# Depthwise convolution block as diagonal matmuls, an fp32 value product on column halves, and shifted loads and stores in a two-layer hybrid trunk

## The chip, the cores and the metric

One core of a Trainium2 chip runs the whole kernel. The metric is device microseconds of one execution. TensorE is PE, its weight loads PEld, VectorE DVE, ScalarE ACT, GpSimd POOL; SP is the queue that issues most DMAs.

## What is computed

Two layers over 1024 tokens of width 1024. Each normalizes, projects once into four mixers, gates each mixer's output, projects back, adds the residual and a gated embedding. The parts that matter here, cut from the reference:

```python
def nsa_attention(q, kc, vc, k_sel, v_sel, k_win, v_win, gates, rel_bias):
    ...
    p_c = masked_softmax(s_c, d_c >= 0)
    o_c = jnp.einsum('bhqn,bnd->bqhd', p_c, vc)
    ...
    o_s = jnp.einsum('bhqm,bqmd->bqhd', p_s, vsel.reshape(B, Q_BLOCK, -1, dk))
    ...
    o_w = jnp.einsum('bhqk,bkd->bqhd', p_w, vw)
    o = gc[..., 0:1] * o_c + gc[..., 1:2] * o_s + gc[..., 2:3] * o_w

def conv_module(a, b, w_dw, b_dw, ln_g, ln_b, w_pw, b_pw):
    x = a * jax.nn.sigmoid(b)
    y = lax.conv_general_dilated(x, w_dw[:, None, :].astype(x.dtype), window_strides=(1,),
                                 padding=((CONV_WIDTH - 1, 0),),
                                 dimension_numbers=('NWC', 'WIO', 'NWC'),
                                 feature_group_count=C) + b_dw
    y = jax.nn.silu(layer_norm(y, ln_g, ln_b))
    return y @ w_pw + b_pw
```

Attention has 4 heads of 64 channels; the convolution has 256 channels and 31 taps. The other mixers are a spatial gating unit and an RWKV-7 recurrence. All is float32.

## The kernel before

Everything is held channel-major, 128 channels by 512 tokens to a tile, and each layer is worked off in two halves of 512 tokens, each half in 4 attention tiles of 128 tokens. `ORDER` (line 32) is written out by hand: one string of steps for each layer and half, run by `run`. The steps that matter: `R` and `r` are the RWKV chunk solve and its serial steps, `N` prepares attention (`nsa_front`, which compresses keys and values in `compress_in` and `compress_out`), `A` is one attention tile, `T` the convolution's taps, `C` what follows them, `O` the output projection, `e` the embedding. The framework's scheduler then interleaves these steps on each engine by priority, within what tiles and PSUM banks allow.

**Dense products** (`mm3`, line 168) are three matmuls over a high and a low part of both operands, in the rounded type that the rows call fp32r. `split_w` (line 150) makes the two parts of each 128x512 piece of weights: ACT rounds it (line 161), POOL subtracts (line 163), and the low part is stored in DRAM (line 165), so that the next half loads it (line 160) and spares POOL.

**The convolution's taps** (`conv_taps`, line 686) run wholly on DVE: for each of two blocks of 128 channels one multiply-add with bias (line 692) and 30 multiply-accumulates (line 695) over 512 tokens. `conv_out` then takes the layer norm's sums on PE as plain fp32 matmuls (line 705), which PE runs as two instructions each.

**An attention tile** (`attn_tile`, line 923; scores and softmax in `branch`, line 987) transposes the probabilities into PSUM tile `pt` (line 969), copies them rounded (ACT, line 972), takes the rest of the rounding (DVE, line 973), and multiplies both with value tiles that hold the high and the low part of v side by side, 128 columns (lines 978 and 979). The two halves of the PSUM tile `pv` are then added (lines 981 and 982) and the gate is multiplied in (line 985). Tiles `pt`, `pv`, `rp` and `c` have one PSUM bank each, `mm` and `s` two.

**DMA issue** is on SP for nearly all: the weights (line 155), the stored low parts, the compression's weights (line 865, 8 loads of 256 KB in each half), the recurrence's state between chunks (line 537, into one buffer `x0`, read by the add of line 551), the embedding's product on its way to DRAM (`ped`, line 1076), and the output (line 1139).

Of the kernel before, what the change touches and what calls it, by code (L numbers as in the profile page):

```python
# [41 lines left out]
class Trunk:  # L42
    def __init__(self, ctx, tc, a):
# [8 lines left out]
        self.low = {}  # L52
        self.setup()

    BUFS = {"aT": 16, "ws": 3, "wh": 3, "wl": 3, "t2": 7, "y": 7, "rv": 2, "pt": 4, "r4": 2, "ab": 8,
# [94 lines left out]
    def split_w(self, src, cols, key):  # L150
        nc = self.nc
        with self.tc.high_priority(offset=4000):
# [9 lines left out]
            if kept is None:  # L162
                nc.gpsimd.tensor_sub(lo[:, :cols], st[:, :cols], hi[:, :cols].bitcast(F32))  # L163
                kept = self.low[key] = self.dram.tile([128, cols], F32, name=f"low{len(self.low)}")
                nc.sync.dma_start(kept, lo[:, :cols].bitcast(F32))
# [8 lines left out]
    def w_granule(self, w2d, k0, nk, segs):  # L174
# [8 lines left out]
        hi, lo = self.split_w(src, nk * n, (w2d.tensor.name, w2d.offset, k0, nk, tuple(segs)))  # L183
# [347 lines left out]
    def rwkv_tri(self, c):  # L531
# [4 lines left out]
        XY = self.t([128, 256], "x0", bufs=1)  # L536
# [149 lines left out]
    def conv_taps(self):  # L686
        nc = self.nc
        par, cw, xg = self.par, self.cw, self.xg
        acc = []
        for j in range(2):  # L690
            ac = self.t([128, 544], "cv")[:, :TH]
            nc.vector.tensor_scalar(ac, xg[j][:, 0:TH], cw[:, j * 31:j * 31 + 1], par[:, P_CB + j:P_CB + j + 1],
# [102 lines left out]
    def nsa_front(self):  # L795
        nc = self.nc
        h = self.h
        im = self.compress_in()
# [14 lines left out]
        VS = self.t([128, NT, 2, 2, 64], "vs", bufs=2, dt=F32R)  # L813
        pv4 = pv.rearrange("p (t s d) -> p t s d", t=NT, s=2)
        nc.scalar.copy(VS[:, :, :, 0, :], pv4)
        nc.vector.tensor_sub(VS[:, :, :, 1, :], pv4, VS[:, :, :, 0, :].bitcast(F32))
# [11 lines left out]
        self.compress_out(*im)  # L828

# [28 lines left out]
    def compress_out(self, im, ns, nn):  # L858
        nc, h = self.nc, self.h
        ph = self.ps("pt")  # L860
        w1 = self.a["nsa_w1"][self.l]
        for kv in range(2):
            for g in range(4):
                w = self.t([128, TH], "ld")
                nc.sync.dma_start(w.rearrange("p (l m) -> p l m", l=4),
                                  w1[kv, g * 512:g * 512 + 512].rearrange("(l p) m -> p l m", p=128))
                for i in range(4):
                    nc.tensor.matmul(ph[32 * i:32 * i + 32, kv * 128:kv * 128 + 128], im[kv][:, g * 4 + i],  # L868
                                     w[:, i * 128:i * 128 + 128], start=(g == 0), stop=(g == 3))
# [28 lines left out]
        self.VC = self.t([128, 2, 64], "vc", bufs=2, dt=F32R)  # L898
        nc.scalar.copy(self.VC[0:64, 0], pt[0:64, 0:64])
        nc.vector.tensor_sub(self.VC[0:64, 1], pt[0:64, 0:64], self.VC[0:64, 0].bitcast(F32))  # L900
        nc.scalar.copy(self.VC[64:128], self.VC[0:64].bitcast(F32))
# [21 lines left out]
    def attn_tile(self, w, t, za):  # L923
# [27 lines left out]
        CS = self.t([128, TH], "pt", dt=F32R)  # L951
        nc.scalar.copy(CS[0:64], pt[0:64])
        nc.vector.tensor_sub(CS[64:128], pt[0:64], CS[0:64].bitcast(F32))
        for hp in range(2):
            pv = self.ps("pv")
            acc = pv[:, :256]
            vc = w.VC.rearrange("p a b -> p (a b)")
            nc.tensor.matmul(acc, vc, CS[:, hp * 256:hp * 256 + 256], start=True, stop=False)
            for br in range(2):
# [3 lines left out]
                for b in range(b0, i + 1, 2):  # L963
# [7 lines left out]
                    Th, Tl = self.t([128, TH], "pt", dt=F32R), self.t([128, TH], "pt", dt=F32R)  # L971
                    nc.scalar.copy(Th[:, :n], pt[:, :n])  # L972
                    nc.vector.tensor_sub(Tl[:, :n], pt[:, :n], Th[:, :n].bitcast(F32))  # L973
                    for x in range(nb):
                        hh, tt = divmod(b + x, NT)
                        vs = w.VS[hh][:, tt, br].rearrange("p a b -> p (a b)")
                        last = br == 1 and b + x == i
                        nc.tensor.matmul(acc, vs, Th[:, x * 256:x * 256 + 256], start=False, stop=False)  # L978
# [343 lines left out]
```

## Time and profile before

| | |
|---|---|
| median of 3 runs | 1896.93 us (1891.67 to 1896.95) |
| the profiled execution | 1898.52 us |
| its span on the core | 1896.8 us, 1.7 us less than its time |
| mean granted clock of PE | 0.93 of 2.4 GHz |
| busy share PE, DVE, ACT, POOL | 89%, 69%, 43%, 20% |
| instructions PE, DVE, ACT, POOL | 9444, 3457, 1837, 311 |

A busy share counts overlapping matmuls as they show in the trace, where each lies some 0.2 us under the next, so PE's share overstates its load: the distance between the starts of neighbours (the pitch) tells what one costs. DMA engines are 50.6% busy with 148 GB/s over the span.

### The profile page before, as it was taken

Reading aid. Unit: us, or ns where it says so; the run is one execution under the profiler, and the core shown is the slowest. Engines: PE = TensorE matmul, PEld = TensorE weight load, DVE = VectorE, ACT = ScalarE, POOL = GpSimd, SP = SyncE. Lnnn points to the kernel's source line nnn. Section 1 sums busy time; section 2 is a strip of 40 time slices with the busy share of each in tenths; the row PEclk is TensorE's granted clock in tenths of the full one; section 3 lists DMA queues with packets and bytes.
Section 4 is the critical chain, followed back from the end, with each engine's and each line's share of the span. In section 5 each row is a group of like instructions: output and inputs, shape, how many; then the busy total and the mean of one; then the engine's idle time right before and its main releaser. Section 6 shows DMA issues by size and latency. Waiting matters only on the chain. (4 is left out here: it accounts for less than half of the span.)

```text
span 1896.8 us, 28498 instructions
## 1 busy us (share of the span) xinstructions
PE 1692.2 (89%) x9444; PEld 1267.9 (67%) x9444; DVE 1306.3 (69%) x3457; ACT 813.4 (43%) x1837; POOL 375.9 (20%) x311
## 2 busy tenths in 40 slices
PE   4886898899799999989968989899988999989998
PEld 3564576677576777767645768676766767667676
DVE  3456689787787756777666883568768876486562
ACT  4332233454333455545322334455532435555553
POOL 2222234000001142312222331200000112422231
PEclk7888799899898999989987989899998989989999
DMA  7456454334664354633364438673365525335566
GB/s 244 101 151 144 126 167 134 99 96 105 168 198 118 85 178 153 212 114 106 110 139 126 146 119 253 200 227 91 109 171 166 148 73 178 116 123 167 164 216 208
DMA packets 382283, 282.16 MB, mean 149 GB/s; under 512 B 94764, under 2 KB 307760, under 8 KB 382136
## 3 DMA queue, kind: packets, MB, share of 16 engines
q1 hardware_dynamic: 382136, 280.34, 50.6%
q8 instruction: 74, 1.21, 0.3%
q14 instruction: 73, 0.60, 0.1%
HBM read 195.72 MB, written 84.54 MB: 148 GB/s over the span
## 5 line engine op out<-in xcount | busy, mean ns | idle before, releaser
L170 PE MATMUL mm<-aT,wh 128*128 128x512 f32 (+1 forms) x1304 | 539.8, 416 | 5.0 <-ACT aT L258 2.8
L171 PE MATMUL mm<-aT,wh 128*128 128x512 f32 (+1 forms) x1304 | 534.9, 411 | 2.7 <-DVE aT L259 2.5
L172 PE MATMUL mm<-aT,wl 128*128 128x512 f32 (+1 forms) x1304 | 535.9, 411 | 1.1 <-DMA wl<-low 1.1
L161 ACT CAST wh<-ws 128x512 fp32r<-128x512 f32 (+2 forms) x388 | 237.1, 612 | 440.0 <-PE mm L171 240.1
L163 POOL TENSOR_TENSOR wl<-ws,wh 128x512 fp32r<-128x512 f32 (+1 forms) x212 | 282.9, 1336 | 697.1 <-ACT wh L161 599.3
L170 PEld LDWEIGHTS mm<-aT,wh 128*128 128x128 f32 (+1 forms) x1304 | 251.6, 193 | 56.5 <-ACT aT L258 4.8
L171 PEld LDWEIGHTS mm<-aT,wh 128*128 128x128 f32 (+1 forms) x1304 | 252.3, 193 | 51.5 <-DVE aT L259 7.7
L172 PEld LDWEIGHTS mm<-aT,wl 128*128 128x128 f32 (+1 forms) x1304 | 251.0, 192 | 49.4 <-DMA wl<-low 1.7
L695 DVE SCALAR_TENSOR_TENSOR cv<-cv,cw,cv 128x512 f32<-128x512 f32 x240 | 191.9, 815 | 3.3
L973 DVE TENSOR_TENSOR pt<-pt,pt 128x512 fp32r<-128x512 f32 (+1 forms) x152 | 94.1, 619 | 99.4 <-ACT pt L972 98.3
L1036 ACT ACTIVATE r<-s,sma 128x512 f32<-128x512 f32 (+3 forms) x192 | 106.0, 554 | 81.7 <-DVE sma L1034 42.2
L972 ACT CAST pt<-pt 128x512 fp32r<-128x512 f32 (+1 forms) x152 | 80.2, 527 | 97.8 <-PE pt L969 97.3
L609 POOL TENSOR_TENSOR q<-SB,gc 128x256 f32<-128x256 f32 x28 | 24.4, 871 | 431.3 <-DMA Xd<-q 152.3
L969 PE MATMUL pt<-cst,r 128*128 128x128 f32 x528 | 98.5, 284 | 12.5 <-DVE r L1041 10.0
L969 PEld LDWEIGHTS pt<-cst,r 128*128 128x128 f32 x528 | 65.5, 145 | 39.3 <-DVE r L1041 18.1
L979 PE MATMUL pv<-pt,vs 128*128 128x256 f32 x264 | 80.3, 322 | 7.8 <-DVE pt L973 7.5
L978 PE MATMUL pv<-pt,vs 128*128 128x256 f32 x264 | 85.7, 325 | 1.1 <-ACT pt L972 0.7
L1006 PE MATMUL s<-kv,qs 128*128 128x512 f32 (+2 forms) x192 | 77.1, 402 | 6.1 <-ACT r L1036 5.8
L979 PEld LDWEIGHTS pv<-pt,vs 128*128 128x128 f32 x264 | 51.4, 195 | 32.9 <-DVE pt L973 27.1
L1041 DVE TENSOR_SCALAR r<-r,sma 128x640 f32<-128x640 f32 (+7 forms) x128 | 72.2, 564 | 0.9
L978 PEld LDWEIGHTS pv<-pt,vs 128*128 128x128 f32 x264 | 51.6, 195 | 31.5 <-ACT pt L972 25.3
L868 PE MATMUL pt<-ld,t 128*32 128x128 f32 x256 | 12.8, 325 | 64.6 <-DMA ld<-in_nsa_w_dram 63.8
(337 smaller groups left out, 2863.8 us busy)
## 6 DMA issues: line engine op xcount, KB each, us to landing
ws<-in_w_in_dram SPq DMA_DIRECT2D x232, 256.0 KB, 3.2
low<-wl SPq DMA_DIRECT2D x200, 256.0 KB, 2.1
wl<-low SPq DMA_DIRECT2D x172, 256.0 KB, 2.8
ws<-in_ple_gate_dram SPq DMA_DIRECT2D x64, 256.0 KB, 3.0
ws<-in_w_out_dram SPq DMA_DIRECT2D x60, 256.0 KB, 3.0
ped<-ot SPq DMA_DIRECT2D x32, 256.0 KB, 3.8
ld<-in_nsa_w_dram SPq DMA_DIRECT2D x32, 256.0 KB, 3.4
ld<-ped SPq DMA_DIRECT2D x32, 256.0 KB, 3.9
```

The source lines that it names most:

```text
L161: nc.scalar.copy(hi[:, :cols], st[:, :cols])
L163: nc.gpsimd.tensor_sub(lo[:, :cols], st[:, :cols], hi[:, :cols].bitcast(F32))
L170: nc.tensor.matmul(out, lh, rh, start=first, stop=False, skip_group_check=shared)
L171: nc.tensor.matmul(out, lh, rl, start=False, stop=False, skip_group_check=shared)
L172: nc.tensor.matmul(out, ll, rh, start=False, stop=last, skip_group_check=shared)
L695: nc.vector.scalar_tensor_tensor(ac, xg[j][:, k:k + TH], cw[:, j * 31 + k:j * 31 + k + 1], ac, op0=OP.mult, op1=OP.add)
L969: nc.tensor.transpose(pt[:, o:o + 128], P[e][:, (b + x - b0) * 128:(b + x - b0) * 128 + 128], self.ident)
L972: nc.scalar.copy(Th[:, :n], pt[:, :n])
L973: nc.vector.tensor_sub(Tl[:, :n], pt[:, :n], Th[:, :n].bitcast(F32))
L978: nc.tensor.matmul(acc, vs, Th[:, x * 256:x * 256 + 256], start=False, stop=False)
L979: nc.tensor.matmul(acc, vs, Tl[:, x * 256:x * 256 + 256], start=False, stop=last)
L1036: nc.scalar.activation(P[:, o:o + wd], p[:, c:c + wd], AF.Exp, bias=ng[:, 0:1], accum_out=den[:, x:x + 1])
```

## The change

1. Of the convolution's two channel blocks, the second goes to PE: for each tap ACT makes a diagonal 128x128 matrix of that tap's weights, and one fp32 matmul over 512 tokens adds it into a PSUM tile `pv`, the bank of the value product. ACT then moves the sum out and adds the bias. 124 matmuls and 124 diagonals in all; 120 + 4 DVE instructions go.
2. The value product is plain fp32: one ACT copy of the transposed probabilities, no DVE remainder, and a matmul of 64 columns for each head, which puts the heads of a pair into the two column halves (partitions 0 to 63 and 64 to 127) of `pv`. One `pv` tile serves a whole attention tile, where before each pair of heads had its own. Lines 981 and 982 fall away, and the gate is one DVE instruction on 128 partitions for each pair.
3. Five of the compression's eight loads are written ahead of `compress_in`.
4. Low parts are stored only where a later half loads them (212 become 152).
5. The stores of `ped` and of the output are issued from ACT's queue.
6. Buffers: `x0` 1 to 2, `r4` 2 to 3, `pt` in SBUF 4 to 3, and `dg` with 4.

```diff
@@ -49,10 +49,10 @@
         self.nd, self.wide, self.xq, self.xs = 0, None, None, None
-        self.low = {}
+        self.low, self.keep = {}, True
         self.setup()
 
-    BUFS = {"aT": 16, "ws": 3, "wh": 3, "wl": 3, "t2": 7, "y": 7, "rv": 2, "pt": 4, "r4": 2, "ab": 8,
+    BUFS = {"aT": 16, "ws": 3, "wh": 3, "wl": 3, "t2": 7, "y": 7, "rv": 2, "pt": 3, "r4": 3, "ab": 8,
             "smr": 6, "sma": 14, "smc": 8, "cv": 4, "ot": 3, "ld": 5, "qa": 1}
@@ -161,6 +161,7 @@
                 nc.gpsimd.tensor_sub(lo[:, :cols], st[:, :cols], hi[:, :cols].bitcast(F32))
+            if kept is None and keep:
                 kept = self.low[key] = self.dram.tile([128, cols], F32, name=f"low{len(self.low)}")
@@ -533,7 +535,7 @@
         cols = [slice(128 * j, 128 * j + 128) for j in range(2)]
-        XY = self.t([128, 256], "x0", bufs=1)
+        XY = self.t([128, 256], "x0", bufs=2)
         nc.sync.dma_start(XY, self.Xcur[:, c * 256:c * 256 + 256])
@@ -687,8 +689,17 @@
         acc = []
+        pq = self.ps("pv")
+        for k in range(31):
+            dg = self.t([128, 128], "dg", bufs=4)
+            nc.scalar.mul(dg, self.ident, cw[:, 31 + k:32 + k])
+            nc.tensor.matmul(pq, dg, xg[1][:, k:k + TH], start=(k == 0), stop=(k == 30))
         for j in range(2):
             ac = self.t([128, 544], "cv")[:, :TH]
+            if j:
+                nc.scalar.activation(ac, pq, AF.Identity, bias=par[:, P_CB + 1:P_CB + 2])
+                acc.append(ac)
+                break
             nc.vector.tensor_scalar(ac, xg[j][:, 0:TH], cw[:, j * 31:j * 31 + 1], par[:, P_CB + j:P_CB + j + 1],
@@ -795,6 +806,7 @@
         h = self.h
+        self.w1 = [self.load_w1(x) for x in range(5)]
         im = self.compress_in()
@@ -810,10 +822,8 @@
             nc.tensor.transpose(pv[:, t * 128:t * 128 + 128], VT[:, t * 128:t * 128 + 128], self.ident)
-        VS = self.t([128, NT, 2, 2, 64], "vs", bufs=2, dt=F32R)
-        pv4 = pv.rearrange("p (t s d) -> p t s d", t=NT, s=2)
-        nc.scalar.copy(VS[:, :, :, 0, :], pv4)
-        nc.vector.tensor_sub(VS[:, :, :, 1, :], pv4, VS[:, :, :, 0, :].bitcast(F32))
+        VS = self.t([128, NT, 2, 64], "vs", bufs=2)
+        nc.scalar.copy(VS.rearrange("p t s d -> p (t s d)"), pv)
         self.VS[h] = VS
@@ -826,6 +836,13 @@
         self.compress_out(*im)
+
+    def load_w1(self, x):
+        kv, g = divmod(x, 4)
+        w = self.t([128, TH], "ld")
+        self.nc.sync.dma_start(w.rearrange("p (l m) -> p l m", l=4), self.a["nsa_w1"][self.l][
+            kv, g * 512:g * 512 + 512].rearrange("(l p) m -> p l m", p=128))
+        return w
 
@@ -858,12 +875,10 @@
         ph = self.ps("pt")
-        w1 = self.a["nsa_w1"][self.l]
         for kv in range(2):
             for g in range(4):
-                w = self.t([128, TH], "ld")
-                nc.sync.dma_start(w.rearrange("p (l m) -> p l m", l=4),
-                                  w1[kv, g * 512:g * 512 + 512].rearrange("(l p) m -> p l m", p=128))
+                x = 4 * kv + g
+                w = self.w1[x] if x < len(self.w1) else self.load_w1(x)
                 for i in range(4):
@@ -948,14 +961,14 @@
             nc.tensor.transpose(pt[0:64, hd * 128:hd * 128 + 128], Pc[:, hd], self.ident)
-        CS = self.t([128, TH], "pt", dt=F32R)
-        nc.scalar.copy(CS[0:64], pt[0:64])
-        nc.vector.tensor_sub(CS[64:128], pt[0:64], CS[0:64].bitcast(F32))
+        CS = self.t([128, TH], "pt")[0:64]
+        nc.scalar.copy(CS, pt[0:64])
+        pv = self.ps("pv")
         for hp in range(2):
-            pv = self.ps("pv")
-            acc = pv[:, :256]
-            vc = w.VC.rearrange("p a b -> p (a b)")
-            nc.tensor.matmul(acc, vc, CS[:, hp * 256:hp * 256 + 256], start=True, stop=False)
+            acc = [pv[64 * e:64 * e + 64, hp * 128:hp * 128 + 128] for e in range(2)]
+            for e in range(2):
+                hd = 2 * hp + e
+                nc.tensor.matmul(acc[e], w.VC, CS[:, hd * 128:hd * 128 + 128], start=True, stop=False, skip_group_check=True)
             for br in range(2):
@@ -968,21 +981,16 @@
                     n = nb * 256
-                    Th, Tl = self.t([128, TH], "pt", dt=F32R), self.t([128, TH], "pt", dt=F32R)
-                    nc.scalar.copy(Th[:, :n], pt[:, :n])
-                    nc.vector.tensor_sub(Tl[:, :n], pt[:, :n], Th[:, :n].bitcast(F32))
+                    PT = self.t([128, TH], "pt")
+                    nc.scalar.copy(PT[:, :n], pt[:, :n])
                     for x in range(nb):
                         hh, tt = divmod(b + x, NT)
-                        vs = w.VS[hh][:, tt, br].rearrange("p a b -> p (a b)")
-                        last = br == 1 and b + x == i
-                        nc.tensor.matmul(acc, vs, Th[:, x * 256:x * 256 + 256], start=False, stop=False)
-                        nc.tensor.matmul(acc, vs, Tl[:, x * 256:x * 256 + 256], start=False, stop=last)
-            tm = self.t([64, 256], "tm", bufs=1)
-            nc.scalar.copy(tm, acc[64:128])
-            nc.vector.tensor_add(tm, acc[0:64], tm)
-            for e in range(2):
-                z = za[hp][64 * e:64 * e + 64, qs]
-                nc.vector.scalar_tensor_tensor(z, tm[:, e * 128:e * 128 + 128], 0.5, z, op0=OP.mult, op1=OP.mult)
+                        for e in range(2):
+                            o = (x * 2 + e) * 128
+                            nc.tensor.matmul(acc[e], w.VS[hh][:, tt, br], PT[:, o:o + 128], start=False,
+                                             stop=br == 1 and b + x == i, skip_group_check=True)
+            z = za[hp][:, qs]
+            nc.vector.scalar_tensor_tensor(z, pv[:, hp * 128:hp * 128 + 128], 0.5, z, op0=OP.mult, op1=OP.mult)
 
@@ -1073,7 +1081,7 @@
             nc.scalar.copy(x, p)
-            nc.sync.dma_start(self.pe_dram[h][b * 128:b * 128 + 128], x)
+            nc.scalar.dma_start(self.pe_dram[h][b * 128:b * 128 + 128], x)
 
@@ -1136,7 +1144,7 @@
         nc.scalar.copy(x, p[:, :w])
-        nc.sync.dma_start(self.a["out"][0, s0:s0 + w, b * 128:b * 128 + 128].rearrange("(t p) c -> p t c", p=128),
+        nc.scalar.dma_start(self.a["out"][0, s0:s0 + w, b * 128:b * 128 + 128].rearrange("(t p) c -> p t c", p=128),
                           x.rearrange("p (t c) -> p t c", c=128))
@@ -1192,6 +1200,7 @@
                 self.h = h
+                self.keep = h == 0
                 mixd = self.mixd = self.mix_dram[h]
@@ -1235,11 +1244,15 @@
                     elif step == "O":
+                        self.keep = out[:2] == (0, 0)
                         prev = self.out_proj(*out)
+                        self.keep = h == 0
                     elif step == "x":
                         prev = self.residual(*prev)
                     elif step == "g":
+                        self.keep = prev[:2] == (0, 0)
                         self.gate_out(*prev)
+                        self.keep = h == 0
                     elif step == "y":
```

Where this puts instructions. In the tables PE's rows are matmuls with output, weights or moving tile, and shape; SP's are DMAs. **PE, third attention tile of layer 0's first half**, before (`mm` and 170 to 172 are the next half's projection, 733 is `conv_out`, the rest is attention):

```order
L170 MATMUL mm_4538<-aT_3607,wh_4541 128x512
L171 MATMUL mm_4538<-aT_3608,wh_4541 128x512
L172 MATMUL mm_4538<-aT_3607,wl_4542 128x512
L978 MATMUL pv_3318<-pt_3407,vs_1182 128x256
L526 MATMUL rp_4340<-cst,ab_4039 128x128
L526 MATMUL rp_4340<-cst,ab_4221 128x128
L170 MATMUL mm_4538<-aT_3612,wh_4541 128x512
L979 MATMUL pv_3318<-pt_3408,vs_1182 128x256
L978 MATMUL pv_3318<-pt_3407,vs_1182 128x256
L979 MATMUL pv_3318<-pt_3408,vs_1182 128x256
L969 MATMUL pt_3415<-cst,r_759_3372 128x128
L969 MATMUL pt_3415<-cst,r_765_3387 128x128
```

The same tile with the change, and what follows it (982 is the transpose, 990 the value product, 944 and 945 the fourth tile's first scores, 696 the convolution):

```order
L982 MATMUL pt_3351<-cst,r_743_3336 128x128
L990 MATMUL pv_3171<-pt_3356,vs_1192 64x128 x4
L982 MATMUL pt_3362<-cst,r_737_3321 128x128
L982 MATMUL pt_3362<-cst,r_743_3336 128x128
L990 MATMUL pv_3171<-pt_3365,vs_1192 64x128 x2
L944 MATMUL pt_3646<-kch_1338,qs_1235 128x64
L945 MATMUL pt_3646<-kcl_1339,qs_1235 128x64
L944 MATMUL pt_3646<-kch_1338,qs_1238 128x64
L945 MATMUL pt_3646<-kcl_1339,qs_1238 128x64
L696 MATMUL pv_3370<-cv_1835,dg_3371 128x512
L696 MATMUL pv_3370<-cv_1835,dg_3374 128x512
L696 MATMUL pv_3370<-cv_1835,dg_3377 128x512
```

No dense row is left among the attention rows here, and the 31 diagonal matmuls stand unbroken behind the tile's last value product; value products come in runs of 2 and 4, two rows to each key block.

**SP, compression's loads of layer 0's first half**, before (497 stores chunk matrices, 537 loads the recurrence's state, `ld` from `in_nsa_w` are the compression's weights):

```order
L497 DMA Xd_85<-q_217_966 32x16x8
L497 DMA Xd_85<-q_219_1013 32x8x16
L865 DMA ld_1316<-in_nsa_w_dram 128x4x128
L865 DMA ld_1322<-in_nsa_w_dram 128x4x128
L750 DMA ld_2190<-in_sgu_wT_dram 128x4x128
L537 DMA x_288_1356<-Xd_85 128x256
L756 DMA ld_2193<-in_sgu_ln_g_dram 128x256
L756 DMA ld_2193<-in_sgu_ln_b_dram 128x256
L760 DMA ld_2196<-in_sgu_b_dram 64x2x128 x2
L729 DMA ld_3530<-in_conv_pw_dram 128x2x256
L865 DMA ld_4772<-in_nsa_w_dram 128x4x128
L537 DMA x_293_1374<-Xd_85 128x256
```

With the change:

```order
L499 DMA Xd_85<-q_217_966 32x16x8
L499 DMA Xd_85<-q_219_1013 32x8x16
L843 DMA ld_1315<-in_nsa_w_dram 128x4x128
L843 DMA ld_1321<-in_nsa_w_dram 128x4x128
L761 DMA ld_2187<-in_sgu_wT_dram 128x4x128
L539 DMA x_288_1353<-Xd_85 128x256
L539 DMA x_293_1371<-Xd_85 128x256
```

The compression's loads stand where they stood, the last two behind the stores of `q`; two loads of the recurrence's state now stand together.

## Rows read from the trace of the kernel before

**Rows 1.** The page's first part: busy time of each engine.

```profile
PE 1692.2 (89%) x9444; PEld 1267.9 (67%) x9444; DVE 1306.3 (69%) x3457; ACT 813.4 (43%) x1837; POOL 375.9 (20%) x311
```

**Rows 2.** Windows: us, busy time (instructions) by engine, PE's clock, DMA share, GB/s.

```profile
200.00:335.00 135.00, 123.86 (x868) 91.49 (x867) 116.77 (x276) 45.42 (x108) 47.70 (x39) 0.95 0.48 141
...
350.00:500.00 150.00, 144.78 (x765) 105.03 (x764) 122.63 (x409) 79.74 (x190) 0.58 (x1) 0.96 0.40 105
```

**Rows 3.** Timeline of PE in dense products: start, duration, line, operation.

```profile
1131.01 0.39 PE L171 MATMUL mm<-aT,wh 128*128 128x512 f32 x1
1131.24 0.39 PE L172 MATMUL mm<-aT,wl 128*128 128x512 f32 x1
```

**Rows 4.** Timeline of PE: plain fp32 matmuls over 512 tokens and the next row.

```profile
1656.20 1.02 PE L705 MATMUL c<-cv,ones 128*128 128x512 f32 x2
1657.06 0.49 PE L950 MATMUL pt<-cst,pc 128*64 128x128 f32 x3
```

**Rows 5.** The same line at another time.

```profile
313.71 1.91 PE L705 MATMUL c<-cv,ones 128*128 128x512 f32 x2
315.42 0.42 PE L648 MATMUL rp<-cst,yt 128*128 128x128 f32 x1
```

**Rows 6.** Windows: an attention tile with no dense product beside it.

```profile
336.00:358.00 22.00, 16.82 (x84) 13.35 (x83) 14.31 (x51) 10.64 (x26) 1.98 (x2) 0.75 0.23 73
```

**Rows 7.** Timeline of PE: half-column matmuls of another step, entry and exit.

```profile
308.06 0.39 PE L172 MATMUL mm<-aT,wl 128*128 128x512 f32 x1
308.38 0.33 PE L785 MATMUL mm<-ld,t 128*64 128x128 f32 x2
...
907.70 1.09 PE L412 MATMUL rp<-cst,smr 128*64 128x128 f32 x16
908.73 0.50 PE L172 MATMUL mm<-aT,wl 128*128 128x512 f32 x1
```

**Rows 8.** Timeline of PE: the value product.

```profile
1365.12 0.27 PE L979 MATMUL pv<-pt,vs 128*128 128x256 f32 x1
1365.23 0.28 PE L978 MATMUL pv<-pt,vs 128*128 128x256 f32 x1
```

**Rows 9.** Groups of DVE by line and shape: busy us, mean ns, idle before.

```profile
L695 DVE SCALAR_TENSOR_TENSOR cv<-cv,cw,cv 128x512 f32<-128x512 f32 x240 | 191.9, 815 | 3.3
L973 DVE TENSOR_TENSOR pt<-pt,pt 128x512 fp32r<-128x512 f32 (+1 forms) x152 | 94.1, 619 | 99.4 <-ACT pt L972 98.3
L953 DVE TENSOR_TENSOR pt<-pt,pt 64x512 fp32r<-64x512 f32 x16 | 11.0, 685 | 6.3 <-ACT pt L952 6.0
L982 DVE TENSOR_TENSOR tm<-pv,tm 64x256 f32<-64x256 f32 x32 | 13.2, 414 | 7.3 <-ACT tm L981 7.3
L985 DVE SCALAR_TENSOR_TENSOR y<-tm,y 64x128 f32<-64x128 f32 x64 | 18.8, 293 | 0.7
```

**Rows 10.** Waits of PE, ACT and PEld: total us, times, longest.

```profile
PE pt L868 <- DMA ld<-in_nsa_w_dram: 63.8, 12, 11.6
ACT r L1036 <- PE pt L969: 31.2, 26, 1.9
PEld pv L979 <- DVE pt L973: 27.1, 60, 3.0
```

**Rows 11.** Timeline of SP at the first compression: start, duration, line, DMA.

```profile
187.40 3.90 SPq L497 DMA_DIRECT2D Xd<-q  x8
191.40 0.95 SPq L865 DMA_DIRECT2D ld<-in_nsa_w_dram  x2
```

**Rows 12.** Waits of SP's queue: total us, times, longest.

```profile
SPq L165 <- POOL wl L163: 535.7, 194, 12.8
...
SPq L537 <- DVE xf L551: 40.2, 20, 5.3
...
SPq L1076 <- ACT ot L1075: 32.1, 15, 8.7
```

**Rows 13.** Groups of ACT: a pass over 512 elements.

```profile
L726 ACT ACTIVATE cv<-cv,cw 128x512 f32<-128x512 f32 x8 | 6.5, 813 | 0.0
```

More of the change, by code (lines that the diff above doesn't have):

```diff
@@ L147, in setup_late, with split_w @@
         nc.vector.tensor_copy(self.TC[:, :, 53:70], pj[:, :68].rearrange("p (a b) -> p a b", a=4))
-    def split_w(self, src, cols, key):
+    def split_w(self, src, cols, key, keep):
         nc = self.nc
@@ L182, in w_granule @@
             o += cn
-        hi, lo = self.split_w(src, nk * n, (w2d.tensor.name, w2d.offset, k0, nk, tuple(segs)))
+        hi, lo = self.split_w(src, nk * n, (w2d.tensor.name, w2d.offset, k0, nk, tuple(segs)),
+                              self.keep)
         v = lambda x: x[:, :nk * n].rearrange("p (k c) -> p k c", k=nk)
@@ L897, in compress_out @@
         nc.tensor.transpose(pt[0:64, 0:64], self.VCT, self.ident[0:64, 0:64])
[L898 to L901, printed above, removed]
+        self.VC = self.t([64, 64], "vc", bufs=2)
+        nc.scalar.copy(self.VC, pt[0:64, 0:64])
     def attention_job(self, za):
```

## The prediction

> **What bounds the kernel now.** I read the page's busy shares first, then windows of single stages, then what the engines wait for. By the page PE is busy 89% of the span and DVE 69% [rows 1], which looks like a kernel bound by PE. It is only half so. In dense products a matmul shows 0.39 us, but the next one starts 0.23 us later [rows 3]: the trace counts overlapping work, and a third of PE's share isn't load. The windows show where DVE counts: in a recurrence stretch, where the convolution's taps run beside it, DVE is busy 117 of 135 us, in an attention stretch 123 of 150, and in the first PE's true load is well under its 124 us [rows 2]. So both engines bind, each in its turn, and the chain between them (transpose on PE, copy on ACT, remainder on DVE, product on PE) sets the rest. Work taken off DVE comes back in part, and work put on PE costs nearly all of itself.
>
> **The change part by part.** The sum is made against the profiled execution, 1898.5 us, 1.6 above the median of the runs; a difference under 0.3%, 5.7 us, can't be told from none.
>
> *Convolution on PE.* Four halves of 31 matmuls, 124. The same operation (plain fp32, 128x512) stands in the trace as pairs of instructions: one matmul moves the next start by 0.86 us at full clock [rows 4] and by 1.71 us at the low level [rows 5]. So 124 x 0.86 = +107 us; bounds 0, if all of it fills time in which PE stands idle, and 124 x 1.71 = +212. I take +107, because the order shows each run unbroken, behind attention tiles whose bank it needs: nothing is woven between that could wait meanwhile.
>
> *Its taps leave DVE.* 120 instructions at 191.9 / 240 = 0.80 us [rows 9] are 96 us. DVE is 86% busy in the stretch where they run [rows 2]; I take 0.7 of it, -67, bounds -24 (a quarter, if PE and the recurrence's chain set that stretch) and -96.
>
> *Diagonals on ACT.* 124 products of 128x128. The nearest row, a pass over 512 elements, takes 0.81 us [rows 13], so each lies between 0 and 0.81, in either case under the 0.86 us that PE needs for one, and four buffers let ACT run ahead. ACT is 43% busy [rows 1]. Zero, as long as PE's run covers them; without that cover up to 124 x 0.81 = 100 us would show.
>
> *Bare attention tiles.* One `pv` tile now serves a whole attention tile, and the convolution needs the same bank. In the order two tiles of each layer's first half have no dense row beside them, four in all, where before dense rows were woven in. One such stretch exists already: in 22 us PE is idle 22.0 - 16.8 = 5.2 us [rows 6]. It was one of these tiles, so three are new: 3 x 5.2 = +16; bounds 0 (the dense rows are only put off) and 3 x 22 = +66.
>
> *Value product on column halves.* Before, 560 matmuls at 0.115 us pitch [rows 8], 64 us. Now 592 of 128 columns; the two heads' halves run as pairs, 296 pairs. An fp32 matmul over 128 columns is a quarter of 0.86, 0.215, so 64 us again. What is new is the entry and the exit. Where another step uses half columns, the first of them starts 0.32 us after the dense matmul instead of 0.23, and its 16 instructions (8 matmuls, 4 pairs) take 1.03 us up to the next row, where 4 x 0.215 = 0.86 would do [rows 7]. That is 0.09 + 0.17 = 0.26 us for a run; the order has 189 runs: 49 us. In attention PE often waits anyway, so I take two fifths, +20, bounds 0 and +49. The Trainium skill speaks against this part of the change: "TensorEngine Tiling (Array Packing)", section Key Properties, says that a change of the tiling mode, not only of the tile, drains the engine. By that rule alone each of 378 changes could cost the 0.39 - 0.23 = 0.16 us that a matmul is still in flight, 60 us, and the sum would come out 11 us higher at its upper bound; the rows show a somewhat smaller loss, and I go by them.
>
> *The remainder leaves DVE.* 94.1 + 11.0 for the remainders, 13.2 for the fold, and half of 18.8 for the gate, together 128 us [rows 9]. Here PE's weight loads waited 27 us for the remainder [rows 10], the lower bound; all of it, -128, is the upper. I take half, -64: the remainder is a link of the chain that attention goes through, but in its place the copy on ACT is last, on which the next transposes wait as well.
>
> *Second buffer for the recurrence's state.* SP waited 40 us for the add that frees `x0` [rows 12], with whatever stood queued behind. I take -16, bounds 0 and -40: the load of the next chunk needs the stored state too, and only some of the 20 waits lie on the path.
>
> *Queues.* 60 of 212 stores of low parts go; SP waits 535.7 / 194 = 2.8 us for POOL at one of them [rows 12], but what is queued behind are loads that run ahead. The `ped` stores leave SP, which waited 32 us for ACT there [rows 12], with the weight loads of the next product behind. Together -10, bounds 0 and -32. The 48 stores on ACT stand right behind their copies and wait for nothing; like the diagonals they cost zero while ACT has room.
>
> *Third score buffer.* ACT waited 31 us for the transposes that free it [rows 10]; off the path as long as PE and DVE are last: 0, bounds 0 and -31.
>
> *Compression's loads early.* PE waited 64 us for them [rows 10]. But in the order five of eight already stood early, and the last two still stand behind the eight stores of `q`: these held the queue for 3.9 us, and both loads went out at 191.4, after them [rows 11]. Nothing moves: 0, bounds 0 and -64.
>
> Sum: 107 - 67 + 16 + 20 - 64 - 16 - 10 = -14, so 1884 for a profiled execution and **1882 us** for the median.
>
> **The rivals.**
>
> *PE becomes the bound (slower).* The place is the attention stretches and the four convolution runs: if PE has no slack there, its whole price counts, 107 + 16 + 49 = 172, less 26 for the queues and the buffer, and of the 224 us taken off DVE only 0.4, 90 us, comes back: +56, 1953 us. It decides from the point at which less than 146 / 224 = 0.65 of DVE's relief comes back. For it: PE's 89% and the bare tiles; against it: the gap between 0.39 and 0.23 us [rows 3], and a DVE that is nearly full in the recurrence.
>
> *DVE is the bound (faster).* Nine tenths of 224 come back, -202; with 107 + 16 + 20 - 26 that is -85, 1812 us. For it: 117 of 135 us [rows 2]. Against it: in the attention stretch PE shows 145 of 150 us.
>
> *The convolution runs at the low clock (slower).* In the bare stretch the granted clock fell to 0.75, and fp32 matmuls there and shortly before took 1.71 us, the 1.2 GHz level [rows 5, 6]. The runs stand right behind such tiles. At that level throughout they cost 105 us more, 1987; for half of each, 1935. Against it: a run of 31 matmuls is itself dense work, and in dense stretches the clock is 0.95 and more [rows 2]. The Trainium skill, "TensorE: Matmul & The Clock Gate", Part 4, says that transposes don't count as busy in the way that products do; by that rule a bare tile, mostly transposes, leaves the clock low for the convolution behind it, and the trace agrees with 0.75 in the one such stretch it has.
>
> *The early loads do take effect (faster).* Then 64 us of waits go, 1818. The order speaks against it; only if the queue reached them earlier for other reasons.
>
> **How the numbers follow.** My forecast has 0.45, PE as the bound 0.28, DVE as the bound 0.17, the low clock 0.06, the loads 0.04. Of the forecast's 0.45 its terms' bounds put 0.30 under the 5.7 us, 0.11 within, 0.04 above; of PE as the bound 0.01 lies within. Faster: 0.30 + 0.17 + 0.04 = 0.51; same: 0.11 + 0.01 = 0.12; slower: 0.04 + 0.27 + 0.06 = 0.37. The range reaches from 1815, which leaves out about half of the DVE case, to 1970, which leaves out the upper third of the PE case and the fully cold clock: some 0.2 together. The forecast's own range is 1855 to 1915.
>
> **What would show it.** Right: 124 fp32 matmuls with a pitch of 0.86 us in four runs of 27 us, DVE's busy time down by some 220 us, PE's waits for the compression's loads still near 64 us, gaps of about 0.1 us at the entry and the exit of the value products. In the recurrence stretches the time should shrink, in the attention stretches stay or grow. The forecast is wrong if the recurrence stretches stay as long with DVE idle in them (then PE or the chain was last), if the convolution's runs show a pitch of 1.7 us, if ACT's diagonals hold PE up, or if the waits for the compression's loads are gone.

## The result, and the profile after

The changed kernel takes 2066.87 us (median of 4 runs, 2064.62 to 2068.59), the kernel before 1894.3 us beside it: a ratio of 1.0924, 95% interval 1.0888 to 1.096. It is 173 us slower. 1882 us with a range up to 1970 was forecast.

The page's busy shares of the changed kernel, which answer to [rows 1]:

```profile
PE 1851.3 (90%) x10316; PEld 1319.6 (64%) x10316; DVE 1128.3 (55%) x3093; ACT 853.3 (41%) x1929; POOL 377.6 (18%) x319
```

DVE lost 178 us of busy time (1306 to 1128; the 224 us counted ahead are durations, and the durations of all its rows fell by 212 us, since rows overlap at their ends), and PE gained 159. Groups of the changed kernel by line and shape, as in [rows 9] (line 696 is the diagonal matmul, two instructions each):

```profile
L696 PE MATMUL pv<-cv,dg 128*128 128x512 f32 x248 | 110.2, 605 | 0.4 <-DVE y L993 0.4
...
L706 DVE SCALAR_TENSOR_TENSOR cv<-cv,cw,cv 128x512 f32<-128x512 f32 x120 | 99.0, 825 | 3.4
...
L993 DVE SCALAR_TENSOR_TENSOR y<-pv,y 128x128 f32<-128x128 f32 x32 | 9.3, 291 | 61.2 <-PE pv L990 61.0
```

The convolution's matmuls wait for almost nothing (0.4 us), and the value product's gate (line 993) is cheap. Two waits that were forecast came too: the first two rows answer to the compression's row in [rows 10], and the third, PE's weight loads waiting for ACT's copy, has taken the place of the remainder's:

```profile
PEld pt L883 <- DMA ld<-in_nsa_w_dram: 64.7, 12, 12.0
...
PE pt L883 <- DMA ld<-in_nsa_w_dram: 59.8, 12, 11.6
...
PEld pv L990 <- ACT pt L985: 55.8, 123, 1.5
```

ACT's diagonals don't hold PE up: ACT waits 58 us for PE at them, and PE's weight loads 1.1 us for ACT.

```profile
L695 ACT ACTIVATE dg<-cst,cw 128x128 f32<-128x128 f32 x124 | 49.0, 400 | 60.1 <-PE pv L696 58.4 <-DVE cw L324 1.7
...
L696 PEld LDWEIGHTS pv<-cv,dg 128*128 128x128 f32 x248 | 47.8, 194 | 60.4 <-issue 58.4 <-ACT dg L695 1.1 <-DVE y L993 0.8
```

So the work that was put on PE costs about what it should, and more time went elsewhere. Windows of the changed kernel (columns as in [rows 2]) show where:

```profile
200.00:335.00 135.00, 126.98 (x876) 94.06 (x877) 97.95 (x247) 46.32 (x110) 45.82 (x39) 0.93 0.48 142
350.00:370.00 20.00, 14.26 (x84) 10.10 (x84) 10.17 (x57) 8.43 (x29) 0.00 (x0) 0.67 0.00 1
370.00:400.00 30.00, 25.73 (x106) 14.87 (x107) 11.04 (x60) 9.46 (x25) 0.00 (x0) 0.50 0.00 1
400.00:428.00 28.00, 27.59 (x66) 12.19 (x65) 0.38 (x1) 12.86 (x32) 0.00 (x0) 0.97 0.00 0
```

In the recurrence stretch DVE is busy 98 of 135 us instead of 117 [rows 2], and PE 127 instead of 124. Then, from 350 to 428 us, the core moves almost no data (DMA share 0.00): PE works through attention tiles alone, its clock granted at 0.67 and then 0.50 of full, and then through 28 us of convolution with DVE idle. Bare is here what has no dense product beside it. PE's dense products (lines 171 to 173) pause from 337.0 to 441.0 us, 104 us, where they paused for 22.6 us before, from 338.7 to 361.2 [rows 6]. The pause's last row before and first row behind, and the timeline of PE around the first convolution:

```profile
337.01 0.39 PE L173 MATMUL mm<-aT,wl 128*128 128x512 f32 x1
...
441.00 1.42 PE L171 MATMUL mm<-aT,wh 128*76 128x512 f32 x1
```

```profile
398.51 0.40 PE L945 MATMUL pt<-kcl,qs 128*128 128x64 f32 x1
398.73 28.42 PE L696 MATMUL pv<-cv,dg 128*128 128x512 f32 x62
426.58 0.59 PE L944 MATMUL pt<-kch,qs 128*128 128x64 f32 x1
```

62 instructions in 27.9 us, 0.90 us a matmul. The next half's norm has its sum ready long before. A row of PE's line 268 (the norm's mean, durations min, median and max, then first and last start), and DVE's timeline, where line 250 takes up first the convolution's variance (`c`), then that mean (`mm`):

```profile
L268 PE MATMUL mm<-onec,qa x8: 167/250/250, 337.9 to 338.6; 128*128 128x1 f32 x8
```

```profile
397.97 0.29 DVE L993 SCALAR_TENSOR_TENSOR y<-pv,y 128x128 f32<-128x128 f32 x1 [5.70 <-PE pv L990]
427.62 0.43 DVE L950 TENSOR_TENSOR pt<-pt,TC 128x256 f32<-128x256 f32 x1 [29.36 <-PE pt L945]
...
432.93 0.16 DVE L250 TENSOR_SCALAR smc<-c 128x4 f32<-128x4 f32 x1 [1.29 <-PE c L726]
433.01 0.14 DVE L1042 TENSOR_REDUCE sma<-sma 128x1 f32<-128x2 f32 x1
433.07 0.15 DVE L250 TENSOR_SCALAR smc<-mm 128x4 f32<-128x4 f32 x1
```

The mean is there at 338.6 us, and DVE touches it at 433.07, one instruction behind the same step of the convolution. For 94 us the next half can't begin, and PE has no dense product. In the second layer's first half it is the same: the mean is there at 1367.7 us, DVE touches it at 1461.02, and the dense products pause for 108 us, where they paused for 13.5 before. The two other convolution runs, at 880 and 1872 us, have no bare stretch ahead of them.

### The profile page after: what moved, and what is told of

Its sections match the earlier page's. It is cut to its first block, busy times and chain, and to the rows that moved or that the text cites. A ratio compares the mean times of both kernels' runs of the same rounds, so it can differ in the third digit from the quotient of the medians.

```text
span 2066.8 us, 29821 instructions
## 1 busy us (share of the span) xinstructions
PE 1851.3 (90%) x10316; PEld 1319.6 (64%) x10316; DVE 1128.3 (55%) x3093; ACT 853.3 (41%) x1929; POOL 377.6 (18%) x319
## 5 line engine op out<-in xcount | busy, mean ns | idle before, releaser
L985 ACT COPY pt<-pt 128x512 f32<-128x512 f32 (+1 forms) x152 | 80.4, 529 | 109.5 <-PE pt L982 108.7
L982 PE MATMUL pt<-cst,r 128*128 128x128 f32 x528 | 109.9, 311 | 6.3 <-DVE r L1049 5.0
L990 PE MATMUL pv<-pt,vs 128*64 128x128 f32 x1056 | 101.2, 308 | 11.2 <-ACT pt L985 10.7
L696 PE MATMUL pv<-cv,dg 128*128 128x512 f32 x248 | 110.2, 605 | 0.4 <-DVE y L993 0.4
L990 PEld LDWEIGHTS pv<-pt,vs 128*64 128x64 f32 x1056 | 60.4, 147 | 64.5 <-ACT pt L985 55.8
L706 DVE SCALAR_TENSOR_TENSOR cv<-cv,cw,cv 128x512 f32<-128x512 f32 x120 | 99.0, 825 | 3.4
L696 PEld LDWEIGHTS pv<-cv,dg 128*128 128x128 f32 x248 | 47.8, 194 | 60.4 <-issue 58.4
L1034 DVE CUSTOM_DVE_ANT_0 s<-s,T 128x256 f32<-128x256 f32 (+1 forms) x144 | 54.3, 379 | 47.5 <-PE s L1015 46.5
L252 POOL TENSOR_TENSOR smc<-smc,mhalf 128x1 f32<-128x1 f32 (+1 forms) x28 | 21.5, 778 | 321.2 <-DVE smc L250 213.4
L695 ACT ACTIVATE dg<-cst,cw 128x128 f32<-128x128 f32 x124 | 49.0, 400 | 60.1 <-PE pv L696 58.4
```

The lines of the kernel that those rows point to most:

```text
L696: nc.tensor.matmul(pq, dg, xg[1][:, k:k + TH], start=(k == 0), stop=(k == 30))
L706: nc.vector.scalar_tensor_tensor(ac, xg[j][:, k:k + TH], cw[:, j * 31 + k:j * 31 + k + 1], ac, op0=OP.mult, op1=OP.add)
L982: nc.tensor.transpose(pt[:, o:o + 128], P[e][:, (b + x - b0) * 128:(b + x - b0) * 128 + 128], self.ident)
L985: nc.scalar.copy(PT[:, :n], pt[:, :n])
L990: nc.tensor.matmul(acc[e], w.VS[hh][:, tt, br], PT[:, o:o + 128], start=False, stop=br == 1 and b + x == i, skip_group_check=True)
```

## The experiments

The **order theory**: the convolution waits in the bank of the value product for three attention tiles, and the next half's norm waits behind the convolution, so PE runs attention bare. Its rival, the **load theory**: PE is full, and the added matmuls and mode changes show whole.

**Both blocks on DVE again.** In `conv_taps` of the changed kernel the loop over diagonals and the branch `if j:` go.

```diff
-        pq = self.ps("pv")
-        for k in range(31):
...
-            if j:
-                nc.scalar.activation(ac, pq, AF.Identity, bias=par[:, P_CB + 1:P_CB + 2])
...
```

> The changed kernel with both convolution blocks on DVE again, all else of the change kept. Order theory (the convolution waits in the bank of the value product for three attention tiles, the norm of the next half waits behind the convolution, and PE runs attention bare meanwhile): about 1870 us, since the bare stretches go with it. Load theory (PE is simply full: 107 us of convolution, 49 us of mode changes and more show whole): 2067 - 107 = 1960 us.

1895.04 us, 1.0028 of before (1.0009 to 1.0047). All the loss hangs on the convolution, and the rest of the change together brings nothing. Page and a window of this run:

```profile
PE 1705.9 (90%) x10068; PEld 1256.0 (66%) x10068; DVE 1204.0 (64%) x3217; ACT 797.3 (42%) x1801; POOL 384.3 (20%) x319
```

```profile
370.00:400.00 30.00, 30.00 (x192) 22.07 (x191) 22.54 (x94) 19.15 (x51) 0.00 (x0) 1.00 0.37 107
```

Where the changed kernel ran bare at half clock, PE here shows full clock and 192 instructions instead of 106. But 1870 was expected: the gains that the prediction gave the value product and the queues are missing.

**Another bank.**

```diff
-        pq = self.ps("pv")
+        pq = self.ps("c1")
```

> The changed kernel with the convolution's sum in the bank c1 instead of pv; same work on every engine. Order theory: the convolution needn't wait for the attention tiles, the bare stretches go: 1890 to 1930 us. Load theory: the same matmuls, 2050 to 2070 us.

1948.49 us, 1.0312 (1.0277 to 1.0348): 118 of the 173 us gone with one word, while PE still does every matmul. It is above the expected 1930, and 53 us over the run with DVE's taps remain. They are the matmuls' price and a rest of the order: the norm's mean comes at 381 us (339 with DVE's taps), and in the first half the dense products still pause for 63.9 us (17.2 with DVE's taps, 104 in the changed kernel). The group (the rows call bank `c1` by `c`) and the same window:

```profile
L696 PE MATMUL c<-cv,dg 128*128 128x512 f32 x248 | 123.9, 609 | 0.0
```

```profile
370.00:400.00 30.00, 27.51 (x144) 17.07 (x143) 15.13 (x71) 17.10 (x48) 1.99 (x2) 0.89 0.00 1
```

In the order the 31 matmuls now stand in 22 pieces between attention rows instead of in one run. The half's third attention tile ends at 403.5 us, where it ended at 398.3 without them: they fill time that attention leaves on PE.

**A tag of its own for the convolution's norm.**

```diff
-        r = self.rstd(pq[:, :NT], NT, 1e-5, "smc")
+        r = self.rstd(pq[:, :NT], NT, 1e-5, "smv")
```

> The changed kernel with one edit: the small tiles of the convolution's layer norm have a tag of their own, so the norm of the next half needn't come after them. The convolution still stands behind the attention tiles. Order theory: the dense rows of the next half fill the bare stretches, 1900 to 1950 us. Load theory: 2050 to 2070 us. If only the place of the convolution counts and not the norm behind it: 2067 us as well, with the bank's run apart from it.

2009.76 us, 1.0639 (1.0594 to 1.0685): 57 us back, less than expected. DVE's line 250 in the same stretch, and windows:

```profile
L250 DVE TENSOR_SCALAR smc<-mm x1: 161/161/161, 338.1 to 338.1; 128x4 f32<-128x4 f32 x1
```

```profile
370.00:400.00 30.00, 30.00 (x205) 21.90 (x202) 16.79 (x89) 15.86 (x45) 0.00 (x0) 1.00 0.31 88
408.00:436.00 28.00, 28.00 (x70) 12.56 (x69) 0.81 (x2) 13.32 (x33) 0.00 (x0) 1.00 0.00 1
```

The norm's step moves from 433 to 338 us, and the bare window becomes a full one. The small tiles of both norms came from one rotating set (`smc`), and both kernels' schedules put the later tile's writer behind the earlier one's; with the tag that order is gone. In the kernel before the convolution was early enough that this cost some 7 us at most (the mean was there at 341 us):

```profile
348.36 0.16 DVE L248 TENSOR_SCALAR smc<-c 128x4 f32<-128x4 f32 x1 [2.04 <-PE c L715]
348.69 0.15 DVE L248 TENSOR_SCALAR smc<-mm 128x4 f32<-128x4 f32 x1
```

What is left is that the convolution still comes late, with nothing beside it (from 408 us on). Its four runs take 26.2 to 26.3 us each, 105 together, most of the 115 us that remain over 1895.

**The convolution alone.** The kernel before with only the diagonals on PE, three buffers for them.

```diff
+        pq = self.ps("pv")
+        for k in range(31):
+            dg = self.t([128, 128], "dg", bufs=3)
...
```

> The kernel before with nothing but the second convolution block on PE, in the bank pv (three buffers for the diagonals instead of four, for space). Order theory: the whole loss is in this part, 2020 to 2070 us. Load theory: 1894 + 107 less what DVE's 96 us give back, 1930 to 2000 us, the rest of the loss coming from the value product's mode changes.

2219.19 us, 1.1742 (1.1706 to 1.1778), 152 us worse than the whole change and well above the expected 2070. Load theory has no place for that: the matmuls are the same. Here attention is slower (its tiles end at 983 us in the first layer's second half, with the change at 880), and the convolution stands behind it. The windows just ahead of it and in it:

```profile
915.00:982.00 67.00, 44.94 (x136) 29.97 (x136) 25.57 (x81) 16.66 (x44) 0.00 (x0) 0.50 0.01 4
982.00:1012.00 30.00, 29.22 (x64) 12.56 (x64) 0.55 (x2) 13.02 (x32) 0.00 (x0) 0.94 0.03 10
```

67 us of bare attention at a clock of 0.50, and then the convolution. The second and third tile of the first half, both bare, take 26 and 39 us here and 20 and 32 in the changed kernel. So the value product's new form, or the third score buffer (they weren't tried apart), does make attention quicker, and that is worth something where everything waits for attention.

**One tap.** The changed kernel with 1 diagonal instead of 31 in each half; 30 taps of the second channel block are left out.

```diff
-        for k in range(31):
+        for k in range(1):
```

> The changed kernel with 1 of the 31 diagonal matmuls and diagonals in each half (30 taps of the second channel block are left out), so the waits for the bank and the order stay and the load of 4 x 30 x 0.86 = 103 us goes. Order theory: the bare attention stays, 2067 - 103 = 1964 us, some 70 above the run with both blocks on DVE (1895). Load theory (bank and tag matter only because the run of matmuls lies behind them): at most 1905 us, as with both blocks on DVE.

1974.57 us, 1.0439 (1.0407 to 1.0472). With almost no matmul left the loss is still 80 us over 1895. So by this run, of the 172 us between 1895 and 2067, 80 are the order and 92 the 120 matmuls (103 by the forecast's pitch of 0.86) with their diagonals. The bare stretch stands as before:

```profile
350.00:370.00 20.00, 14.29 (x76) 10.24 (x76) 10.06 (x55) 8.41 (x29) 0.00 (x0) 0.63 0.01 1
370.00:400.00 30.00, 23.54 (x108) 13.97 (x110) 12.18 (x63) 10.37 (x32) 0.00 (x0) 0.53 0.00 1
```

**Both cures.** Bank `c1` and the tag.

> The changed kernel with both cures: the convolution's sum in the bank c1, and its layer norm's small tiles under a tag of their own. If both waits cost by themselves: under 1940 us (1948 with the bank alone). If the bank's wait was the only one that the norm inherited: 1945 to 1952 us, and 53 us above both blocks on DVE are the price of the matmuls themselves, half of their 107 us.

1943.39 us, 1.0277 (1.0253 to 1.0301): 5 us under the bank alone, about what the two runs' spread can tell, and between the two expectations. With the bank alone the norm's mean waits 9 us for the convolution (381 to 390 us), with both cures 1 us. That it comes at 381 us and not at 339 is left, and so is a pause of 52.5 us in the dense products; what holds it there isn't shown.

**Taps early.** Bank `pv` kept, the steps `c` and `T` written ahead of the attention tiles.

```diff
-ORDER = ("iXeHFBRNrGabscdnAAATCy",
+ORDER = ("iXeHFBRNrGabscTdnAAACy",
...
```

> The changed kernel, bank pv kept, with the step of the taps written ahead of the half's attention tiles in ORDER (and the gate that it takes along). Order theory: another way to the same cure as the bank c1, 1930 to 1970 us. Load theory: 2050 us and more.

1987.99 us, 1.051 (1.048 to 1.054), above the expected 1970. 79 us come back, the size of the order's part, and 93 over 1895 stay, the size of the 120 matmuls' part. No long bare stretch is left in the first half (the dense products pause for 19.6 and 17.3 us). The convolution stands in 4 to 25 pieces in a half, but ahead of the attention tiles and between rows of other steps, dense products and the recurrence above all. So it isn't the pieces that hide half of the price in bank `c1`, but the attention rows beside them.

**The queues alone.** The kernel before with the change's stores, queues, `x0` and early loads.

> The kernel before with only the fewer stored low parts, the stores on ACT's queue, the second buffer x0 and the early loads; convolution on DVE and value product as before. The prediction's terms for these: -16 - 10 = -26, 1864 us. Rival: SP's waits and x0 lie off the path, 1885 to 1895 us.

1881.14 us, 0.9947 (0.9928 to 0.9966): -10 of the forecast -26, between the two expectations.

**The value product alone.**

> The kernel before with only the value product in fp32 on column halves. The prediction's terms for it: -64 + 20, 1846 us. Rival: PE is the bound there and its mode changes eat what DVE gives, 1880 to 1900 us. If bare attention tiles come from the one pv tile alone, above 1900 us.

1906.5 us, 1.0084 (1.0063 to 1.0105): +16 where -44 was forecast. -10 and +16 make the +5 of both blocks on DVE. A time above 1900 was also the sign of bare tiles from the one `pv` tile, but there are none: the dense products pause for 20.8 us in the first half, 22.6 before. PE's timeline at one product, and its wait:

```profile
399.83 0.40 PE L172 MATMUL mm<-aT,wl 128*128 128x512 f32 x1
400.16 0.66 PE L973 MATMUL pv<-pt,vs 128*64 128x128 f32 x8
400.75 0.44 PE L965 MATMUL pt<-cst,r 128*128 128x128 f32 x2
```

```profile
PEld pv L973 <- ACT pt L968: 50.2, 121, 1.4
```

The first of the eight half-column instructions starts 0.33 us after the dense matmul. Over all such pairs in the trace the median is 0.326 us where the full-width value product had 0.235, and from a value product to the next transpose 0.203 where it had 0.118: 0.09 + 0.09 us for a run. And the wait for the remainder (27 us) and the copy (25 us) has become one of 50 us for the copy.

**Taps left out.** The kernel before without 30 taps of the second block, and nothing in their place.

```diff
-            for k in range(1, 31):
+            for k in range(1, 1 if j else 31):
```

> The kernel before without 30 of the 31 taps of the second channel block (left out of the computation), so DVE loses 96 us and PE gets nothing. The prediction's term: -67, 1824 us. If half comes back, as the 53 us between the convolution in bank c1 and both blocks on DVE suggest: 1838 us. If PE sets the recurrence's stretches too: above 1870 us.

1907.61 us, 1.0086 (1.0054 to 1.0118). 75 us less of DVE's busy time (1306 to 1231) bring nothing; the kernel is even slower. The recurrence stretch, beside the first row of [rows 2]:

```profile
200.00:335.00 135.00, 127.18 (x877) 94.84 (x878) 98.69 (x251) 46.87 (x110) 44.62 (x39) 0.93 0.49 142
```

DVE falls from 117 to 99 us, PE's rows leave 8 us idle instead of 11, and the first attention scores behind the stretch come at 290.5 us instead of 294.7: 4 us for 30 taps. Whether PE's work or the recurrence's chain sets the stretch wasn't tried apart.

**The remainder left out.** PE multiplies the high part twice; the low part of the probabilities is left out.

```diff
-                    Th, Tl = self.t([128, TH], "pt", dt=F32R), self.t([128, TH], "pt", dt=F32R)
+                    Th = Tl = self.t([128, TH], "pt", dt=F32R)
...
-                    nc.vector.tensor_sub(Tl[:, :n], pt[:, :n], Th[:, :n].bitcast(F32))
```

> The kernel before without DVE's remainder of the rounding in the value product: PE multiplies the high part twice instead, so that PE and ACT do the same work and DVE loses 94 us (the low part of the probabilities is left out of the computation). The prediction's term for it and the fold: -64, which would be about 1840 us here. Rival, that the copy on ACT takes the remainder's place as the last link: 1875 to 1890 us, and then the fp32 column halves cost PE the rest up to 1906 us.

1901.24 us, 1.0068 (1.0043 to 1.0094). Nothing comes back, which is beyond what the rival expected. PEld's wait for the copy, in the kernel before and here:

```profile
PEld pv L978 <- ACT pt L972: 25.3, 96, 1.1
```

```profile
PEld pv L977 <- ACT pt L972: 29.2, 100, 1.1
```

The 27 us of waits for the remainder are gone and those for the copy grew from 25 to 29, so the copy didn't take the remainder's place as the rival had it: the waits went and the time stayed. The value product in fp32 stands at 1.0084 (1.0063 to 1.0105) and this run at 1.0068 (1.0043 to 1.0094); the intervals overlap, so a net cost of the half columns, some 3 us by the ratios, can't be told from none.

**Early loads that are early.** The queues alone, with the compression's loads on ACT's queue.

```diff
-        self.nc.sync.dma_start(w.rearrange("p (l m) -> p l m", l=4), self.a["nsa_w1"][self.l][
+        self.nc.scalar.dma_start(w.rearrange("p (l m) -> p l m", l=4), self.a["nsa_w1"][self.l][
```

> The kernel before with the queues, stores, x0 and written-early loads of the change (1881 us), and the compression's loads issued from ACT's queue, so that the last three needn't stand behind the stores of q on SP. If PE's 64 us of waits for them lie on the path: 1820 to 1850 us. If something else is last there (the buffers of the loads, the recurrence): 1875 to 1885 us with PE's waits for these loads down to some 30 us or unchanged.

1853.73 us, 0.9793 (0.9771 to 0.9816), less than both kernels and the queues' run take, and 4 us above the expected range. PE's wait for these loads in the queues' run, and here:

```profile
PE pt L876 <- DMA ld<-in_nsa_w_dram: 63.7, 12, 11.4
```

```profile
PE pt L876 <- DMA ld<-in_nsa_w_dram: 8.3, 7, 2.2
```

55 us of waits went and 27 us of time; the first attention scores come at 266 us instead of 286. SP's queue also lost 32 loads, which wasn't tried apart.

**Queues with the tag.**

> The kernel before with the queues, stores and x0 of the change (1881 us), and a tag of its own for the small tiles of the convolution's layer norm. If the norm of the next half waits for the convolution also where its taps run on DVE: 1860 to 1875 us. If that order only cost where the convolution itself was late: 1878 to 1885 us.

1882.72 us, 0.9938 (0.9914 to 0.9963): no difference to 1881. With the taps on DVE the convolution isn't late enough for the order to show in the time.

## Why the prediction was wrong

**The bare tiles, +16, bounded by +66.** This step failed, and it failed in its mechanism. It priced only PE's idle share inside three attention tiles, and that from a window which is hardly a tile: of the 84 instructions of PE in [rows 6] 28 are attention's, 12 are dense products, and most others are the convolution's sums and the norm's. The order it quoted showed the convolution behind the tiles' bank; what it didn't ask is what stands behind the convolution. There stood the next half's norm, tied to it by the tag `smc`, and with it all dense work and the loads for it. The runs put about 80 us on this (one tap 80, taps early 79), and the tag alone gives 57 back.

**The convolution on PE, +107.** Right in size (0.90 us a matmul in the first run, 92 of 103 us with the order apart), and rightly taken whole: 93 us are left in the run with the taps early, where no long bare stretch is. Only between attention rows (bank `c1`) is it less, 53 us with a rest of the order in them.

**DVE's relief, -67 and -64.** The second failed step. DVE's 117 of 135 us were read as a bound. Taking 96 us of taps away gave +0.9%, taking the remainder away +0.7%. In the recurrence stretch PE stays busy and 4 us come back; in attention the fp32 product waits for ACT's copy instead, 50 us where copy and remainder had 52, as the prediction itself noted before it took half. Even with the remainder left out, where these waits fell to 29 us, no time came back. So over the whole kernel none of the relief came back, far under the 0.65 below which the first rival decides. Without the two relief terms and with 80 for the order, the prediction's own sum is 1898 + 107 + 80 + 20 - 26 = 2079.

**Mode changes, +20 of 49.** An entry of 0.09 us was right, the exit is 0.09 and not 0.17: 189 runs make 34 us, and what shows of them can't be told from none. The Trainium skill, "TensorEngine Tiling (Array Packing)", section Key Properties, says that a change of mode drains the engine. The trace agrees in kind, since each change costs time; the measured 0.09 us is under the 0.16 us that a matmul is still in flight.

**Queues and `x0`, -26.** Right in sign, -10 measured.

**Diagonals, 0, and third score buffer, 0.** The diagonals were right: 0.40 us each, and PE doesn't wait for them. The buffer wasn't tried by itself; the two runs without it add up to +6 us and the run with it is at +5, which leaves it nothing to show.

**The compression's loads, 0.** Right: 59.8 us of waits against 63.8 [rows 10]. Once they really left early they were worth 27 us, inside the bound of 64.

**The rivals.** The slower one, PE as the bound, had the side right, and its 0.4 of relief was still too kind. The low clock came in another place than named: in the bare tiles, at 0.67 and 0.50, and not in the convolution, which ran at 0.97. The Trainium skill, "TensorE: Matmul & The Clock Gate", Part 4, says that transposes don't count as busy like products. No run here shows whether that is the reason: a bare tile isn't mostly transposes, as the rival took it, since of PE's 187 instructions between 350 us and the convolution 48 are transposes, 43 scores and 96 value products. Against the rival's fear the clock was back within the convolution's run. How much of the 80 us is the clock and how much PE's waiting wasn't tried apart.

Still open: why the kernel grows slower, by 0.7 and 0.9%, when DVE only loses work. The scheduler orders every engine's rows anew for such an edit; which of the new places costs the time isn't shown.

## What to carry to other kernels

Before work is moved to another engine, look up whose buffers it will take and what is next in line for its own: a PSUM bank or a small rotating tag that two steps share puts one behind the other, and a step that was early by chance becomes late with everything behind it. A high busy share of an engine in a stretch isn't a bound: leave its work out once and see whether the stretch gets shorter. Where an engine waits for loads that are "written early", see in the queue's order what stands ahead of them; another queue may be the whole cure.

## What the runs showed of the hardware

The granted clock fell to the 1.2 GHz level, 0.50, during 30 us of attention without dense products, with PE's rows showing it busy for 26 of them, and it was at 0.97 over the 28 us of convolution behind. Half-column fp32 matmuls of two heads do run beside each other: the eight instructions of the value product's timeline, four matmuls, start in pairs 0.007 us apart and take 0.59 us up to the next transpose, where four of 128 columns one after the other would take 4 x 0.215 = 0.86 by an estimate from the row of 0.86 us for 512 columns [rows 4]. The step into the half columns and the step out cost 0.09 us each, next to a full-width value product in the same places.
